# Moving four z tiles into the paired products, the norm products to VectorE and the norm rows to GpSimd's queue

## The chip, the cores and the metric

The kernel runs on one core of a Trainium2 chip. The metric is the device time of one execution in microseconds (us). A core has five engines that run side by side, each in the order of its own queue: TensorE (PE: matmuls, with PEld for its weight loads), VectorE (DVE), ScalarE (ACT), GpSimd (POOL) and SyncE (SP), which here only issues transfers (DMAs).

## The reference, cut to what matters

```python
u = rmsnorm(x) @ w_in                      # x: 1024 x 1024
z, xbc, dt_raw, s_b, s_c, s_x, g_a, g_b = split(u)     # z: 1024 x 2048
xbc = silu(conv4(xbc) + b);  xs, bm, cm = split(xbc)
y = ssd_chunked_scan(xs, softplus(dt_raw + dt_bias), a, bm, cm) + d_skip * xs
y = y * silu(z)
y = y * rsqrt(mean over each of 4 groups of 512 (y * y) + EPS) * ssd_norm_w
branch_a = y @ w_ssd_proj
branch_b = (s_b * conv3(s_c * s_x)) @ w_sconv_proj
h = x + (sigmoid(g_a) * branch_a + sigmoid(g_b) * branch_b) @ w_o
out = rmsnorm(h + swiglu(rmsnorm(h)))
```

All is float32. Each product is made of three matmuls (high by high, high by low, low by high) of rounded halves of both operands.

## The kernel before, in words

`u` is kept transposed: a tile is 128 columns of `w_in` by 1024 rows of `x`. Most tiles are made two at a time by a product of seven terms in place of eight (class `Pair`): a pair takes 7 slots of 4 matmul triples, 84 matmuls of 128x512, and leaves two tiles. The others, 6 tiles of z and the 16 gate tiles, are made one at a time in `direct_tile`: 2 halves of 8 triples, 48 matmuls a tile (lines L81 to L83, tile `pr`). The stages:

1. **Start.** The first four row tiles of `x` are loaded, squared and summed (L115, L117), scaled by their norm (L135, L137, tile `xn`), transposed on PE (L1542, tile `pt`), taken out of PSUM by `turned_out` (L1549 on ACT, L1551 on DVE, tile `br`) and split into high and low halves (L76, L77: `th`, `tl`). `cols` holds the small per-channel vectors; its copy is L1534.
2. **Pairs.** 29 pairs, 7 slots each (L679 to L681, tiles `pb` and `pd`). Ten of the 16 z tiles are here. A little way in, `d_skip_columns` (L1643) spreads the skip weights on DVE (L1644, `rd`) and transposes them on PE (L1646).
3. **Direct tiles and scan**, about 600 to 961 us. 22 direct tiles. Between their triples `pump_scan` puts the 65 steps of the scan (4 groups of 8 chunks, a step `part1` and a step `part2` for each), spread evenly over the triples by `due`. A step has small matmuls (`pxt`, `pcb`, `poff`, `pst`, `pdg`), a dozen DVE instructions and ACT's decays. Every four chunks a generator `norm` starts; it goes on by one `yield` at each scan step: it loads two tiles of silu(z) (L507), multiplies y by them (L513, on POOL), squares (L517, L518 on ACT: `sa`), adds (L520, L521 on DVE), sums over partitions on PE (L526, `pq`), takes the root (`rstd_of`, L99 to L107, with the square root on ACT, L101), transposes the result (L531, `prt`), copies it (L533, `rst`), writes it to memory (L535) and reads it back spread over 128 partitions (L537, `rbc`, from SP's queue), scales y by it (L543) and, for a second half, forms sums for the next product (L557).
4. **Merge.** Products of seven terms over weights and activations read back (class `Chunk`, `Stream`; `gb`, `gd` on PE; `split`, L73 to L77, makes `gh`, `gl`, `qh`, `ql`). The end of the last two norms runs beside its first chunks: after chunk 1, 2, 3 and 4 the program takes 4, 3, 0 and 3 scan steps.
5. The gated feed-forward and the last norm.

There is no scheduler: each engine's order is that of the program. Tiles come from a pool of 47 pages, and a load waits until the page's former content is read.

Of the kernel before, what the change touches and what calls it, by code (L numbers as in the profile page):

```python
# [10 lines left out]
AF = mybir.ActivationFunctionType  # L11
ALU = mybir.AluOpType

P = 128
S = 1024
D = 1024
# [23 lines left out]
def hybrid_block(ctx: ExitStack, tc: tile.TileContext, x, nmw, w_in, cw, cb, dtb, alog, dsk, snw,  # L40
                 wssd, scw, wsc, wo, nfw, wg, wu, wd, fnw, out):
    nc = tc.nc
    ET = mybir.EngineType
    ctx.enter_context(tc.manual_schedule(engines={ET.PE, ET.Activation, ET.DVE, ET.Pool, ET.SP}))
    x, w_in, out = x[0], w_in[0], out[0]
# [10 lines left out]
    def nm(s):  # L56
        cnt[0] += 1
        return f"{s}_{cnt[0]}"

    def page(s, shape=(P, 1024), dt=F32):  # L60
        return pp.tile(list(shape), dt, tag="pg", name=nm(s))

    def bank(s):
        return sm.tile([P, 512], F32, tag="sm", name=nm(s))
# [31 lines left out]
    def rstd_of(ssq, n, s):  # L96
        shp = list(ssq.shape)
        v = sp.tile(shp, F32, tag="rv", name=nm(s + "v"))
        nc.vector.tensor_scalar(v, ssq, 1.0 / n, EPS, op0=ALU.mult, op1=ALU.add)  # L99
        r = sp.tile(shp, F32, tag="rr", name=nm(s + "r"))  # L100
        nc.scalar.activation(r, v, AF.Sqrt)  # L101
        nc.vector.reciprocal(r, r)
        q = sp.tile(shp, F32, tag="rq", name=nm(s + "q"))
        nc.vector.tensor_mul(q, r, r)
        nc.vector.tensor_mul(q, q, v)
        nc.vector.tensor_scalar(q, q, -0.5, 1.5, op0=ALU.mult, op1=ALU.add)
        nc.vector.tensor_mul(r, r, q)  # L107
        return r
# [17 lines left out]
            rows_sq_on(e, acc, s)  # L126
        return acc

    def rows_scale(src, xn, ssq, act=(), pool=()):
        r = rstd_of(ssq, D, "n")  # L130
        for i in range(len(src)):
            if i in pool:
                nc.gpsimd.tensor_scalar(xn[i], src[i], r[:, i:i + 1], 1.0, op0=ALU.mult, op1=ALU.mult)
            elif i in act:
                nc.scalar.activation(xn[i], src[i], AF.Copy, scale=r[:, i:i + 1])  # L135
            else:
                nc.vector.tensor_scalar_mul(xn[i], src[i], r[:, i:i + 1])  # L137
        return xn

    def fill(rows, raw, half, wcol):  # L140
# [33 lines left out]
    def wslab(w, c0, cols=P, r0=0):  # L174
        return Slab(w[r0:r0 + D, c0:c0 + cols].rearrange("(k p) f -> p k f", p=P), (P, KT, cols))
# [45 lines left out]
    def every(gen):  # L221
        for _ in gen:
            pass
# [22 lines left out]
    d2 = cp.tile([16, 2], F32, name="d2")  # L246
# [9 lines left out]
    rd = cp.tile([16, 2, 64], F32, name="rd")  # L256
    cols = cp.tile([P, 192], F32, name="cols")
# [30 lines left out]
    V = nc.vector  # L288
# [213 lines left out]
    def norm(g, hf, y0, y1):  # L502

        ys, o = (y0, y1), slice(hf * 512, hf * 512 + 512)
        for i in range(2):
            z = page("z", HB)
            nc.sync.dma_start(z, z_g[g][256 * i:256 * i + 256, o].rearrange("(r p) l -> p r l", p=P))  # L507
            if i == 0:
                zs = z
        yield  # L510
        yield
        for y, z in zip(ys, (zs, z)):
            nc.gpsimd.tensor_mul(y, y, z)  # L513
        yield
        yield
        sa, sb = page("sa", HB), page("sa", HB)
        nc.scalar.activation(sa, y0, AF.Square)  # L517
        nc.scalar.activation(sb, y1, AF.Square)  # L518
        yield
        V.tensor_add(sa, sa, sb)  # L520
        V.tensor_add(sa[:, 0], sa[:, 0], sa[:, 1])  # L521
        yield
        yield
        pq = bank("pq")
        for c in range(4):
            nc.tensor.matmul(pq[:, c:c + 1], sa[:, 0, c * P:(c + 1) * P], ones, start=True, stop=True)  # L526
        rs = rstd_of(pq[:, 0:4], INNER // G, "g")
        yield
        yield
        prt = bank("prt")  # L530
        nc.tensor.transpose(prt[:4, :P], rs, ident)  # L531
        rst = sp.tile([4, P], F32, tag="rst", name=nm("rst"))
        nc.scalar.activation(rst, prt[:4, :P], AF.Copy)  # L533
        rd_ = rs_d[2 * g + hf]
        nc.sync.dma_start(rd_, rst)  # L535
        rbc = page("rbc", (P, 512))
        nc.sync.dma_start(rbc, rd_.rearrange("c l -> (c l)").partition_broadcast(P))  # L537
        yield
        yield
        yield  # L540
        for r in range(4):
            z = ys[r // 2][:, r % 2]
            V.scalar_tensor_tensor(z, z, snc(4 * g + r), rbc, op0=ALU.mult, op1=ALU.mult)  # L543
            if r % 2:
                yield
                if hf == 0 or r > 1:
                    nc.sync.dma_start(y_g[g][128 * (r - 1):128 * (r + 1), o].rearrange("(r p) l -> p r l", p=P),
                                      ys[r // 2])
        if hf == 0:
            kept[g] = ys  # L550
            return

        b11, b21 = kept.pop(g)
        b12, b22 = ys
        t1, t2 = page("s1", HB), page("s2", HB)
        for t, a, b, f in ((t1, b11, b12, "T1"), (t2, t1, b22, "T2"), (b12, b12, b22, "T3"), (b21, b21, t2, "T4")):
            V.tensor_add(t, a, b)  # L557
            nc.sync.dma_start(yt_d[f][256 * g:256 * g + 256, :].rearrange("(k p) f -> p k f", p=P), t)
            yield
# [50 lines left out]
    def silu_z(i):  # L610
        def f(u):
            nc.scalar.activation(u, u, AF.Silu)
            nc.scalar.dma_start(z_d[i], u)
            yield
        return f
# [290 lines left out]
                side.append(self.done[1](self.u2))  # L906
                self.u2 = self.b = None

    z_pairs = [Pair(i * P, (silu_z(i), silu_z(i + 1))) for i in range(0, 10, 2)]
    x_pairs = [Pair(XBC0 + i * P, (conv_silu(i), conv_silu(i + 1))) for g in range(G)  # L910
               for i in (4 * g, 4 * g + 2)]
    bc_pairs = [Pair(XBC0 + i * P, (conv_silu(i), conv_silu(i + 1))) for i in (16, 18, 20, 22)]
# [13 lines left out]
    NF = len(first)  # L926
# [33 lines left out]
    z_held = []  # L960

    def z_raw(i):
        def f(ps, hf):
            if hf == 0:
                z_held.append((i, page("gt")))
            nc.scalar.activation(z_held[-1][1][:, hf * 512:hf * 512 + 512], ps, AF.Copy)
            if hf and len(z_held) == 3:
                for k, t in z_held:
                    nc.scalar.activation(t, t, AF.Silu)
                    nc.scalar.dma_start(z_d[k], t)  # L970
                z_held.clear()
        return f

    direct = [(wslab(w_in, i * P), z_raw(i)) for i in range(10, 16)]
    for j in range(KT):
        direct += [(wslab(w_in, GA0 + j * P), gate_raw(ga_d[j])), (wslab(w_in, GB0 + j * P), gate_raw(gb_d[j]))]
    scan_steps = scans()
# [550 lines left out]
    a0 = rows_sq(xt[0:4], "x", "avav")  # L1528
    a1 = rows_acc(xt[4:8], "x")
    del xt  # L1530
    pc = bank("pc")
    nc.tensor.transpose(pc[:, 0:96], ra, ident[:96, :96])
    nc.tensor.transpose(pc[:, 96:176], rb, ident[:80, :80])
    nc.vector.tensor_copy(cols[:, 0:176], pc[:, 0:176])  # L1534
    r0 = rows_scale(*a0, act=(3,))
    raw0, raw1 = ([], []), ([], [])
    turned = {}

    def turn_rows(rows, k):
        pt = turned[k] = bank("pt")  # L1540
        for i in range(4):
            nc.tensor.transpose(pt[:, i * P:(i + 1) * P], rows[i][:, k * P:(k + 1) * P], ident)  # L1542

    def turned_out(raw, k):
        if k % 2 == 0:
            raw[k // 4].append(page("br", HB))
        o, pt = raw[k // 4][-1][:, k % 2, :], turned.pop(k)
        if k % 2 == 0:
            nc.scalar.activation(o, pt, AF.Copy, scale=nmc[:, k:k + 1])  # L1549
        else:  # L1550
            V.tensor_scalar_mul(o, pt, nmc[:, k:k + 1])  # L1551

    p0, p1, p2 = first
    for k in range(4):
        turn_rows(r0, k)
    turned_out(raw0, 0)
    turned_out(raw0, 1)
    p0.hi("A1")
    turned_out(raw0, 2)
    turned_out(raw0, 3)  # L1560
    p0.lo("A1")
# [78 lines left out]
            pump()  # L1640
    every(gen)

    def d_skip_columns():  # L1643
        V.tensor_copy(rd, d2.unsqueeze(2).to_broadcast([16, 2, 64]))  # L1644
        pd2 = bank("pd2")
        nc.tensor.transpose(pd2[:, 0:16], rd.rearrange("a b c -> a (b c)"), ident[:16, :16])  # L1646
        V.tensor_copy(cols[:, 176:192], pd2[:, 0:16])
# [3 lines left out]
    for i in range(7 * NF, n_slots):  # L1651
        slot(i)
        if i == 7 * NF + 4:
            time_steps(steps_ps)
            del steps_ps[:]
        if i == 7 * NF + 14:
            d_skip_columns()
        make(i)
        load_pairs((i + 11) // 7 + 1)
        pump()  # L1660
        if i % 3 == 0:
            next(sums, None)
        if i % 3 == 1:
            pump_aux()
        left = n_slots - 1 - i
        if left in (4, 3, 2):
            del T[{4: "T2", 3: "T1", 2: "T3"}[left]]
        if left == 9:
            b12 = [page("br", HB) for _ in range(2)]
            for k in range(2):  # L1670
                nc.sync.dma_start(b12[k], b12_d[k])
        if left == 7:
            direct[0][0].load()
        if left == 4:
            every(put("B12", b12))
        if left == 3:
            direct_hi(direct[0][0])
            direct[1][0].load()
        if left == 2:
            direct_lo(direct[0][0])  # L1680
            pump_scan()
# [42 lines left out]
```

## Time and profile before

| | us |
|---|---|
| median of 3 runs (lowest, highest) | 1929.16 (1929.04, 1929.68) |
| the profiled execution | 1931.04 |
| span of the profile, first to last instruction | 1929.3 |

A row of a group or a timeline names engine, line, operation, the tiles out<-in and the shape. In a timeline the two first numbers are start and duration in us, and what stands in brackets is the idle time ahead of it and what ended it. Matmuls overlap: the duration of one is longer than the distance to the next, so time on PE is counted by distances. Rows of waits give total, times and longest. A row of stretches gives for each engine its busy time in the stretch and the number of instructions.

### The profile page before, as it was taken

To read this page: it belongs to the slowest core of one execution; us is meant where nothing else is said; L and a number is where in the kernel's file an instruction comes from. 1 tells how busy PE (TensorE), PEld (TensorE's weight loads), DVE (VectorE), ACT (ScalarE), POOL (GpSimd) and SP (SyncE) were. 2 spreads that over 40 slices of the span, in tenths; PEclk is the share of its full clock that TensorE was granted. 3 is DMA by queue.
4 is the path that set the end of the run, shared out by engine and by line. 5 is a ranking of instruction groups with operands and counts; after the bars stand their busy time and mean duration, and the time that the engine had idled before them with its cause. 6 is when DMAs were issued, how large, how long until landed. Compare 5 with 4: busy or idle time off the path is not lost.

```text
span 1929.3 us, 24107 instructions
## 1 busy us (share of the span) xinstructions
PE 1887.9 (98%) x8917; PEld 1550.9 (80%) x8917; DVE 1291.1 (67%) x1660; ACT 965.0 (50%) x1533; POOL 181.4 (9%) x168
## 2 busy tenths in 40 slices
PE   7999999999999999999989999999999999999998
PEld 5688888888887888888868888887888888888886
DVE  7667878677774868887878548877444444456465
ACT  5545454444446877777546454465333333345333
POOL 1010111010100101010100000101221121100000
PEclk9999999999999999999989999999999999999999
DMA  5297999988959557768669766736998788867562
GB/s 179 62 260 170 242 233 232 229 207 227 272 138 289 189 180 252 246 220 275 209 243 373 233 222 203 207 125 133 227 205 208 199 192 200 217 259 287 193 196 109
DMA packets 345094, 411.97 MB, mean 214 GB/s; under 512 B 17192, under 2 KB 223744, under 8 KB 344976
## 3 DMA queue, kind: packets, MB, share of 16 engines
q1 hardware_dynamic: 293232, 325.39, 51.7%
q0 software_dynamic: 43680, 55.67, 18.2%
q10 hardware_dynamic: 8064, 29.36, 3.8%
q8 instruction: 70, 1.15, 0.2%
q14 instruction: 48, 0.39, 0.1%
HBM read 320.56 MB, written 143.15 MB: 240 GB/s over the span
## 4 chain that ended last, share of the span: by engine, by line
PE 87%; DVE 6%; ACT 3%; DMA 2%; issue 1%; SPq 0%; ACTq 0%; DVEq 0%
PE pb L679 5%; PE pb L680 5%; PE pb L681 5%; PE gb L680 5%; PE gb L679 5%; PE gb L681 5%; PE fb L681 4%; PE fb L679 4%; PE fb L680 4%; PE pr L81 4%; PE pr L83 4%; PE gd L679 4%; PE gd L680 4%; PE gd L681 4%; PE pr L82 4%; PE pd L679 4%
## 5 line engine op out<-in xcount | busy, mean ns | idle before, releaser
L77 DVE TENSOR_TENSOR wl<-ws,wh 128x1024 fp32r<-128x1024 f32 x77 | 94.0, 1222 | 121.5 <-ACT wh L76 121.5
L680 PE MATMUL gb<-ql,gh 128*128 128x512 f32 x432 | 169.7, 393 | 3.2 <-DVE ql L77 3.2
L679 PE MATMUL gb<-qh,gh 128*128 128x512 f32 x432 | 169.6, 393 | 1.1 <-DVE h L1132 1.1
L681 PE MATMUL gb<-qh,gl 128*128 128x512 f32 x432 | 169.3, 392 | 0.0
L81 PE MATMUL pr<-th,wh 128*128 128x512 f32 x352 | 144.2, 410 | 0.0
L83 PE MATMUL pr<-th,wl 128*128 128x512 f32 x352 | 138.2, 393 | 2.0 <-DVE wl L990 2.0
L681 PE MATMUL fb<-th,wl 128*128 128x512 f32 x352 | 137.2, 390 | 0.8 <-DVE wl L77 0.8
L679 PE MATMUL fb<-th,wh 128*128 128x512 f32 x352 | 137.3, 390 | 0.6 <-ACT wh L76 0.6
L82 PE MATMUL pr<-tl,wh 128*128 128x512 f32 x352 | 137.5, 391 | 0.0
L680 PE MATMUL fb<-tl,wh 128*128 128x512 f32 x352 | 137.1, 390 | 0.0
L679 PE MATMUL gd<-qh,gh 128*128 128x512 f32 x324 | 127.0, 392 | 0.0
L680 PE MATMUL gd<-ql,gh 128*128 128x512 f32 x324 | 126.7, 391 | 0.0
L681 PE MATMUL gd<-qh,gl 128*128 128x512 f32 x324 | 126.7, 391 | 0.0
L77 DVE TENSOR_TENSOR ql<-cb,qh 128x1024 fp32r<-128x1024 f32 x98 | 118.0, 1204 | 2.6 <-ACT qh L76 2.5
L76 ACT ACTIVATE qh<-cb 128x1024 fp32r<-128x1024 f32 x98 | 99.9, 1019 | 38.4 <-PE gb L680 17.2
L679 PE MATMUL fd<-th,wh 128*128 128x512 f32 x264 | 102.8, 390 | 0.0
L681 PE MATMUL fd<-th,wl 128*128 128x512 f32 x264 | 102.8, 390 | 0.0
L680 PE MATMUL fd<-tl,wh 128*128 128x512 f32 x264 | 102.8, 389 | 0.0
L74 DVE SCALAR_TENSOR_TENSOR gl<-ca,gh 128x1024 fp32r<-128x1024 f32 (+1 forms) x60 | 72.8, 1214 | 44.4 <-ACT gh L73 44.4
L680 PEld LDWEIGHTS gb<-ql,gh 128*128 128x128 f32 x432 | 81.8, 189 | 20.7 <-DVE ql L77 3.9
L679 PEld LDWEIGHTS gb<-qh,gh 128*128 128x128 f32 x432 | 81.8, 189 | 18.7 <-DVE h L1132 1.4
L681 PEld LDWEIGHTS gb<-qh,gl 128*128 128x128 f32 x432 | 81.9, 189 | 16.9
(319 smaller groups left out, 4681.7 us busy)
## 6 DMA issues: line engine op xcount, KB each, us to landing
ws<-in_w_in_dram SPq DMA_DIRECT2D x80, 512.0 KB, 7.1
ws<-in_w_gate_dram SPq DMA_DIRECT2D x77, 256.0 KB, 3.9
ws<-in_w_up_dram SPq DMA_DIRECT2D x77, 256.0 KB, 4.4
ca<-u_d SPq DMA_DIRECT2D x35, 512.0 KB, 5.5
ab<-ac_d SPq DMA_DIRECT2D x32, 512.0 KB, 6.9
xbc_g<-cv ACTq DMA_DIRECT2D x24, 512.0 KB, 7.0
ws<-ws POOLq DMA_DIRECT2D x22, 512.0 KB, 6.5
wd_d<-in_w_down_dram SPq DMA_DIRECT2D x20, 512.0 KB, 9.8
```

What stands on the lines that cost most here:

```text
L74: nc.vector.scalar_tensor_tensor(lo, src, -1.0, hi.bitcast(F32), op0=ALU.mult, op1=ALU.subtract)
L76: nc.scalar.activation(hi, src, AF.Copy)
L77: nc.vector.tensor_sub(lo, src, hi.bitcast(F32))
L81: nc.tensor.matmul(o, lh, rh, start=first, stop=False)
L82: nc.tensor.matmul(o, lh, rl, start=False, stop=False)
L83: nc.tensor.matmul(o, ll, rh, start=False, stop=last)
L679: nc.tensor.matmul(o, lh, rh, start=first, stop=False, skip_group_check=True)
L680: nc.tensor.matmul(o, lh, rl, start=False, stop=False, skip_group_check=True)
L681: nc.tensor.matmul(o, ll, rh, start=False, stop=last, skip_group_check=True)
```

## The change

Seven edits in one diff.

- `z_pairs` takes tiles 0 to 13 in place of 0 to 9: two more pairs (at the end of the pairs), four fewer direct tiles, 18. Only z tiles 14 and 15 stay direct, and their silu is done after two tiles instead of three (`z_raw`). The 65 scan steps are spread over the 18 tiles, since `due` goes by their number.
- In `norm` the product with silu(z) (L513) is on VectorE.
- In `norm` both transfers of the norm row (L535, L537) are issued from GpSimd's queue.
- In the start, `rows_scale` goes by column halves: first columns 0 to 511 of the four rows, then 512 to 1023.
- In the start, the copy of `cols` (L1534) is on ScalarE.
- In the start, the high half of the first weights (`p0.hi`, L864) stands ahead of the first two `turned_out`.
- `d_skip_rows` (the DVE copy L1644) is one slot ahead of `d_skip_columns`.

```diff
-    def rows_scale(src, xn, ssq, act=(), pool=()):
+    def rows_scale(src, xn, ssq, act=(), parts=1):
         r = rstd_of(ssq, D, "n")
-        for i in range(len(src)):
-            if i in pool:
-                nc.gpsimd.tensor_scalar(xn[i], src[i], r[:, i:i + 1], 1.0, op0=ALU.mult, op1=ALU.mult)
-            elif i in act:
-                nc.scalar.activation(xn[i], src[i], AF.Copy, scale=r[:, i:i + 1])
-            else:
-                nc.vector.tensor_scalar_mul(xn[i], src[i], r[:, i:i + 1])
+        for c in range(parts):
+            cs = slice(c * D // parts, (c + 1) * D // parts)
+            for i in range(len(src)):
+                if i in act:
+                    nc.scalar.activation(xn[i][:, cs], src[i][:, cs], AF.Copy, scale=r[:, i:i + 1])
+                else:
+                    nc.vector.tensor_scalar_mul(xn[i][:, cs], src[i][:, cs], r[:, i:i + 1])
         return xn
...
         for y, z in zip(ys, (zs, z)):
-            nc.gpsimd.tensor_mul(y, y, z)
+            V.tensor_mul(y, y, z)
...
-        nc.sync.dma_start(rd_, rst)
+        nc.gpsimd.dma_start(rd_, rst)
         rbc = page("rbc", (P, 512))
-        nc.sync.dma_start(rbc, rd_.rearrange("c l -> (c l)").partition_broadcast(P))
+        nc.gpsimd.dma_start(rbc, rd_.rearrange("c l -> (c l)").partition_broadcast(P))
...
-    z_pairs = [Pair(i * P, (silu_z(i), silu_z(i + 1))) for i in range(0, 10, 2)]
+    z_pairs = [Pair(i * P, (silu_z(i), silu_z(i + 1))) for i in range(0, 14, 2)]
...
-            if hf and len(z_held) == 3:
+            if hf and len(z_held) == 2:
...
-    direct = [(wslab(w_in, i * P), z_raw(i)) for i in range(10, 16)]
+    direct = [(wslab(w_in, i * P), z_raw(i)) for i in range(14, 16)]
...
-    nc.vector.tensor_copy(cols[:, 0:176], pc[:, 0:176])
-    r0 = rows_scale(*a0, act=(3,))
+    nc.scalar.activation(cols[:, 0:176], pc[:, 0:176], AF.Copy)
+    r0 = rows_scale(*a0, act=(3,), parts=2)
...
+    p0.hi("A1")
     turned_out(raw0, 0)
     turned_out(raw0, 1)
-    p0.hi("A1")
     turned_out(raw0, 2)
     turned_out(raw0, 3)
     p0.lo("A1")
...
+    def d_skip_rows():
+        V.tensor_copy(rd, d2.unsqueeze(2).to_broadcast([16, 2, 64]))
+
     def d_skip_columns():
-        V.tensor_copy(rd, d2.unsqueeze(2).to_broadcast([16, 2, 64]))
...
+        if i == 7 * NF + 13:
+            d_skip_rows()
         if i == 7 * NF + 14:
             d_skip_columns()
```

How the order moves at the three places that the prediction speaks of. First VectorE where the merge begins: `gl` and `ql` are the low halves for its second and third chunk, `y_7640` and `y_7641` are the y of the last norm, `y_7175` that of the one before. Before:

```order
L107 TENSOR_TENSOR gr_8123<-gr_8123,gq_8126 128x4
L557 TENSOR_TENSOR y_6719<-y_6719,y_6720 128x1024
L74 SCALAR_TENSOR_TENSOR gl_8178<-ca_7882,gh_8177 128x1024
L77 TENSOR_TENSOR ql_8182<-cb_7884,qh_8181 128x1024
L77 TENSOR_TENSOR gl_8186<-ca_8032,gh_8185 128x1024
L77 TENSOR_TENSOR ql_8190<-cb_8034,qh_8189 128x1024
L557 TENSOR_TENSOR y_6256<-y_6256,s_1231_8078 128x1024
L543 SCALAR_TENSOR_TENSOR y_7175<-y_7175,cols,rbc_8228 128x512 x2
L520 TENSOR_TENSOR sa_8232<-sa_8232,sa_8233 128x1024
```

The same place of the changed kernel, in which the last norm's y are `y_7691` and `y_7692`, and `y_7250` is that of the one before:

```order
L107 TENSOR_TENSOR gr_8138<-gr_8138,gq_8141 128x4
L557 TENSOR_TENSOR y_6819<-y_6819,y_6820 128x1024
L74 SCALAR_TENSOR_TENSOR gl_8190<-ca_7864,gh_8189 128x1024
L77 TENSOR_TENSOR ql_8194<-cb_7866,qh_8193 128x1024
L77 TENSOR_TENSOR gl_8198<-ca_8044,gh_8197 128x1024
L77 TENSOR_TENSOR ql_8202<-cb_8046,qh_8201 128x1024
L557 TENSOR_TENSOR y_6388<-y_6388,s_1237_8096 128x1024
L513 TENSOR_TENSOR y_7691<-y_7691,z_8146 128x1024
L513 TENSOR_TENSOR y_7692<-y_7692,z_8148 128x1024
L543 SCALAR_TENSOR_TENSOR y_7250<-y_7250,cols,rbc_8240 128x512 x2
L520 TENSOR_TENSOR sa_8244<-sa_8244,sa_8245 128x1024
```

The two products stand between the splits of the third chunk and the scaling that waits for the norm row. Second, SP's queue at the same time: `ca` and `cb` are the merge's operands, `yt_d` takes the last of the sums (L557), and `rs_d_138` and `rbc_8228` are the norm row of the norm before the last. Before:

```order
L741 DMA cb_8175<-vt_d_160 128x2x512
L558 DMA yt_d_166<-y_6256 128x2x512
L535 DMA rs_d_138<-rst_8225 4x128
L537 DMA rbc_8228<-rs_d_138 128x512
L741 DMA ca_8240<-sc_d_144 128x2x512
L741 DMA cb_8242<-vt_d_160 128x2x512
```

GpSimd's queue of the changed kernel from the same norm to the first instruction of the feed-forward (`ws`):

```order
L535 DMA rs_d_138<-rst_8237 4x128
L537 DMA rbc_8240<-rs_d_138 128x512
L535 DMA rs_d_139<-rst_8401 4x128
L537 DMA rbc_8404<-rs_d_139 128x512
L1239 DMA ws_10141<-in_w_gate_dram 128x4x128
```

The norm row no longer stands behind the store of y, and the loads of the merge no longer behind the norm row. Third, ScalarE at the start: `xn_213` is the fourth row tile, `wh` the high half of the first weights, `br` and `th` the transposed rows and their high halves. Before:

```order
L101 ACTIVATE nr_222<-nv_220 128x4
L135 ACTIVATE xn_213<-x_88,nr_222 128x1024
L1549 ACTIVATE br_254<-pt_234,cols 128x512
L864 ACTIVATE wh_257<-ws_183 128x1024
L1549 ACTIVATE br_260<-pt_244,cols 128x512
L76 ACTIVATE th_284<-br_254 128x1024
```

And of the changed kernel:

```order
L1534 ACTIVATE cols<-pc_216 128x176
L101 ACTIVATE nr_222<-nv_220 128x4
L135 ACTIVATE xn_213<-x_88,nr_222 128x512 x2
L864 ACTIVATE wh_258<-ws_183 128x1024
L1549 ACTIVATE br_261<-pt_238,cols 128x512
L1549 ACTIVATE br_264<-pt_248,cols 128x512
L76 ACTIVATE th_288<-br_261 128x1024
```

The weights' half stands ahead of both transposed tiles, and the copy of `cols`, which was on VectorE ahead of the root, is here.

## The prediction

> **What bounds the kernel now.** I read the page first, then PE's waits, then the stretches of the scan stage, then the timelines of the two places where PE stands.
>
> ```profile
> span 1929.3 us, 24107 instructions
> PE 1887.9 (98%) x8917; PEld 1550.9 (80%) x8917; DVE 1291.1 (67%) x1660; ACT 965.0 (50%) x1533; POOL 181.4 (9%) x168
> L81 PE MATMUL pr<-th,wh 128*128 128x512 f32 x352 | 144.2, 410 | 0.0
> PE pc L1532 <- DMA ra<-in_ssd_conv_w_dram: 7.4, 1, 7.4
> PE pq L526 <- DVE sa L521: 6.4, 1, 6.4
> PE gb L680 <- DVE ql L77: 3.2, 1, 3.2
> PE pr L83 <- DVE wl L990: 2.0, 3, 1.1
> PE pd L1646 <- DVE rd L1644: 0.8, 1, 0.8
> 300.00:400.00 100.00, 100.00 (x441) 82.58 (x441) 75.62 (x86) 44.27 (x58) 8.82 (x10) 1.00 0.83 203
> 600.00:720.00 120.00, 116.58 (x689) 94.54 (x688) 78.22 (x129) 97.29 (x222) 11.36 (x5) 1.00 0.65 204
> 720.00:961.00 241.00, 241.00 (x1472) 199.10 (x1471) 201.27 (x336) 172.29 (x398) 24.81 (x10) 1.00 0.73 240
> 961.00:1000.00 39.00, 29.45 (x112) 23.52 (x112) 25.26 (x28) 18.37 (x23) 5.70 (x2) 0.82 0.74 255
> ```
>
> PE bounds: it is busy for 98% and a matmul starts every 100/441 = 0.227 us. It stands only at the start and at 961 to 1000, where 112 matmuls take the time of 39/0.227 = 172: some 13 us are lost there, part of it to a granted clock of 0.82. The scan stage is full on PE, but VectorE is at 201.3 of 241 us in its main stretch, so it is next.
>
> **The change, part by part.** The sum is made on the profiled execution: 1931.0 us in all, span 1929.3. The runs' median, 1929.2, has no profile; I carry the difference over to it.
>
> *Matmuls.* Four direct tiles are 4 x 48 = 192 (the group shows 352 = 22 x 16 for one of three lines), two pairs are 2 x 84 = 168. 24 fewer at 0.227: **-5.4**. The pair stage grows by 38.1, the scan stage loses 43.5.
>
> ```profile
> 500.00:600.00 100.00, 100.00 (x442) 82.60 (x441) 72.84 (x84) 44.92 (x59) 10.36 (x12) 1.00 0.81 216
> ```
>
> What a pair needs beside its matmuls (sums and splits on VectorE, halves and evictions on ScalarE, two loads of 512 KB) is costed at nothing: the last 100 us of pairs keep PE full with VectorE at 73% and ScalarE at 45%, and four z tiles have no convolution, which most pairs there carry. Were that cover gone, a pair would take as long as VectorE's work on it, still under its 19 us of matmuls by the same row.
>
> *Start.*
>
> ```profile
> 11.96 2.08 DVE L137 TENSOR_SCALAR xn<-x,nr 128x1024 f32<-128x1024 f32 x3
> 14.10 4.90 PE L1542 MATMUL pt<-ident,xn 128*128 128x128 f32 x30 [0.19 <-DVE xn L137]
> 17.29 0.75 DVE L1551 TENSOR_SCALAR br<-pt,cols 128x512 f32<-128x512 f32 x1 [0.86 <-PE pt L1542]
> 20.36 0.50 PE L680 MATMUL pb<-tl,wh 128*128 128x512 f32 x1 [1.13 <-DVE tl L77]
> 19.84 0.42 ACT L1512 ACTIVATE wdt<-wdts 128x256 fp32r<-128x256 f32 x1 [0.65 <-DMA wdts<-in_w_in_dram]
> 10.27 0.34 DVE L1534 COPY cols<-pc 128x176 f32<-128x176 f32 x1
> ```
>
> Three whole rows take VectorE 2.08 us, so the three first halves are there after about 1.04, and the transposes run through 1.0 earlier; the copy that leaves VectorE gives 0.3 more; the weights' half on ScalarE fills its wait instead of standing between tiles. So PE's 20.36 comes 1.3 to 1.7 earlier. But `wdts` still lands at 19.84, and ScalarE stops there with all that follows. Kept to the end: 0.6 to 1.7, taken **-1.0**.
>
> *Skip rows.* The copy goes a slot ahead; its wait (0.8) goes, and VectorE has the same work: **-0.8**, at worst 0.
>
> *Waits at direct tiles.* PE waited three times for `wl`, 2.0 in all; one ACT silu group of three is now one of two, the other gone. 0 to 2.0, taken **-0.5**.
>
> *End of the norms, 961 to 1000.*
>
> ```profile
> 963.56 3.47 DVE L74 SCALAR_TENSOR_TENSOR gl<-ca,gh 128x1024 fp32r<-128x1024 f32 x1 [4.12 <-ACT gh L73]
> 966.95 3.37 DVE L77 TENSOR_TENSOR ql<-cb,qh 128x1024 fp32r<-128x1024 f32 x1
> 970.24 1.21 DVE L77 TENSOR_TENSOR gl<-ca,gh 128x1024 fp32r<-128x1024 f32 x1
> 963.53 5.70 POOL L513 TENSOR_TENSOR y<-y,z 128x1024 f32<-128x1024 f32 x2 [33.34 <-ACT gh L73]
> 967.01 0.27 ACT L533 ACTIVATE rst<-prt 4x128 f32<-4x128 f32 x1 [0.64 <-PE prt L531]
> 973.75 0.36 SPq L558 DMA_DIRECT2D yt_d<-y  x1
> 974.21 0.32 SPq L535 DMA_DIRECT2D rs_d<-rst  x1
> 981.55 1.41 DVE L543 SCALAR_TENSOR_TENSOR y<-y,cols,rbc 128x512 f32<-128x512 f32 x2 [7.82 <-DMA rbc<-rs_d]
> 984.97 1.84 PE L526 MATMUL pq<-ones,sa 128*128 128x1 f32 x8 [6.38 <-DVE sa L521]
> ```
>
> While POOL multiplies, two VectorE splits take 3.47 and 3.37 instead of 1.21: 4.4 us, and PE's 3.2 wait behind `ql`. With the products on VectorE, behind these splits, that goes. Then the norm row: ready at 967.3, it waited in SP's queue for a store until 974.21, and VectorE had it 7.3 later. From GpSimd, which has nothing else queued, it leaves at 967.3. How long that queue takes for it no row shows:
>
> ```profile
> ra<-in_ssd_conv_w_dram POOLq DMA_DIRECT2D x1, 48.0 KB, 5.5
> ws<-in_w_up_dram POOLq DMA_DIRECT2D x22, 256.0 KB, 8.0
> ```
>
> The ends are SP's own 7.3 and 5.5 + 8.0 = 13.5 by POOL's rows. I take 8.5, near the first, for the transfer is the same, and the second row's is one that adds up. So `rbc` at 975.8 (974.6 to 980.8), and `pq` 3.4 later as now, at 979.2 instead of 984.97: -5.8; half a microsecond back for VectorE's two products ahead of it: **-5.3** (-0.7 to -7.3). A wait of PE remains here, since its second chunk, no longer held, ends near 972: some 7 us, with its price in clock.
>
> ```profile
> 970.96 0.63 PE L681 MATMUL gb<-qh,gl 128*128 128x512 f32 x1
> 971.39 0.63 PE L679 MATMUL gb<-qh,gh 128*128 128x512 f32 x1
> ```
>
> After the first wait the matmuls go at 0.43 instead of 0.227 for a while; that loss lies before `pq` and goes with the wait. After `pq` I leave it as it is, since a wait of about the same length stands ahead of it in both kernels.
>
> The Trainium skill's "DMA: Bandwidth & Descriptors", section "SWDGE vs HWDGE vs iDMA", speaks against this edit: plain transfers belong on SP or ACT, where hardware makes the descriptors. By its first-byte figures (about 1 and 0.6 us, section "Specifications") two transfers would cost 0.8 more than on SP, an estimate of 8.1 in place of my 8.5; no run here shows it yet.
>
> In the other norms GpSimd waits for `rst` with nothing queued behind it, and SP, which had waited there, is free.
>
> *VectorE in the scan stage.* 16 products come to VectorE's queue, 14 of them in this stage, and a product now holds back all scan work behind it if its z is late.
>
> ```profile
> L513 POOL TENSOR_TENSOR y<-y,z 128x1024 f32<-128x1024 f32 x16 | 41.0, 2584 | 323.9 <-DMA z<-z_g 175.1 <-DVE y L496 39.5 <-DVE wl L990 39.3
> L557 DVE TENSOR_TENSOR s<-y,y 128x1024 f32<-128x1024 f32 x4 | 4.9, 1218 | 0.0
> 925.00 5.20 POOL L513 TENSOR_TENSOR y<-y,z 128x1024 f32<-128x1024 f32 x2 [36.63 <-DMA z<-z_g]
> 927.27 3.21 DVE L496 TENSOR_TENSOR y<-y,xx 128x256 f32<-128x256 f32 x2
> 919.58 0.76 DVE L496 TENSOR_TENSOR y<-y,xx 128x256 f32<-128x256 f32 x2
> DVE gr L102 <- ACT gr L101: 19.3, 6, 4.3
> DVE xx L437 <- PE pxt L426: 8.0, 5, 2.9
> ```
>
> Z is in time: POOL starts at 925.00, and VectorE reaches this place only after 927.27. The stretch of 241 us shrinks with the stage, (361 - 43.5)/361, to 212. VectorE's work in it: 201.3, less 2.4 (3.21 against 0.76) for each pair of products that collides, taken for three of the five pairs, -7.4, plus ten products at 1.2, +12, less three weight splits, -3.6: 202, or 95%. In line with it stand 19.3 us of waits for ScalarE's square root; with them 222, 10 over. PE's waits for a scan step's state come only when VectorE is two steps, 2 x 212/43 = 10 us, behind (65 steps in 317 us, 43 here). So between 0 and 10 us reach PE; taken **+2**, near the low end, since VectorE starts this stretch with 78.2 of 120 us used.
>
> Sum: -5.4 - 1.0 - 0.8 - 0.5 - 5.3 + 2 = -11.0, so 1929.2 - 11.0 = **1918.2**.
>
> **The rivals.**
>
> *All covers hold.* VectorE stays ahead and every term is at its good end: -5.4 - 1.7 - 0.8 - 2.0 - 7.3 = -17.2: 1912. For it: PE had no wait at all in the 241 us, and VectorE's collisions may have cost more than the 7.4 I took off. Against it: the 222 needs the whole lag of 10 to stay hidden.
>
> *VectorE gives the matmuls back.* It falls 8 us behind instead of 2: -5.0, 1924.2. For it: the 222 against 212.
>
> *GpSimd's queue is as slow as its rows.* 13.5 instead of 8.5: the end gives 0.7 instead of 5.3: -6.4, 1922.8. Against it: those transfers met full queues.
>
> *Both:* -0.4, 1928.8, no change.
>
> *Slower: VectorE bounds the scan stage.* If all its idle time (241 - 201.3 = 39.7) is order of work and moves along, it needs 202 + 39.7 = 242 where PE has 212, so 30 come on top of -13.0: 1946. It decides from 17 us of PE waits in this stage. Against it: part of the idle time was waiting for PE (`pxt`, 8.0), which goes when VectorE is late.
>
> **How the numbers follow.** Forecast 0.48, all covers 0.17, matmuls back 0.14, slow queue 0.08, both 0.06, slower 0.07. A measurement tells about 0.2%, 3.9 us. The first four are faster by more (0.87), both is within (0.06), the last slower (0.07). The range leaves out these last two, 0.13, and a little of the far end of the covers: 1911.5 to 1924.5.
>
> **What would show it.** Matmuls with `pr` 864 instead of 1056. VectorE's `gl` and `ql` at the merge's begin at 1.2 us each; `pq` there with a wait of 3 to 7, some 6 us sooner after the first `gb`; `rs_d` and `rbc` 8 to 9 us from `rst` to VectorE. VectorE over 90% busy in the scan stage, its wait for `pxt` nearly gone, and PE's waits there for `st`, `xw` or `wl` some 2 us. The first `tl` matmul near 19. Wrong if PE's waits in the scan stage pass 8 us, or if the norm row takes over 12.

## The result and the profile after

| us | before | after |
|---|---|---|
| median (lowest, highest) of 6 runs each | 1929.84 (1929.04, 1931.28) | 1942.72 (1939.96, 1943.55) |
| the profiled execution | 1931.04 | 1939.96 |
| span of the profile | 1929.3 | 1938.2 |

The ratio is 1.0064, interval 1.0051 to 1.0077. The forecast was 1918.2, so the kernel is 12.9 us slower where 11 less were expected. The profiled execution is the quickest of the six; the working below is made on its span, 8.9 above that of before.

The head of the page of after, and the group of one of the three lines of direct tiles:

```profile
span 1938.2 us, 24072 instructions
PE 1886.9 (97%) x8893; PEld 1547.4 (80%) x8893; DVE 1304.7 (67%) x1698; ACT 966.2 (50%) x1540; POOL 149.0 (8%) x168
L81 PE MATMUL pr<-th,wh 128*128 128x512 f32 x288 | 120.3, 418 | 0.0
```

The matmuls did go: 288 = 18 x 16 for each line, 24 fewer on PE in all. But PE is busy for nearly as long, 1886.9 against 1887.9, in a span that is 8.9 longer. Where it stands now, from PE's waits in the whole of after, without those of the start:

```profile
PE pq L526 <- DVE sa L521: 11.2, 2, 9.2
PE prt L531 <- DVE gr L107: 5.4, 4, 2.4
PE pr L83 <- DVE wl L990: 3.8, 1, 3.8
PE poff L475 <- DVE st L484: 2.1, 1, 2.1
```

Every one of them names VectorE (two smaller ones, 1.1 and 0.9, name ScalarE). Three of the four lie in the scan stage, and so do 2.0 of the first; before, all listed waits of PE between 637 and 961 came to 0.5. The stretches of after from the first direct tile (637) to the first `gb` (974) and beyond show when it happens:

```profile
637.00:760.00 123.00, 122.13 (x756) 99.81 (x755) 91.58 (x157) 104.47 (x251) 1.13 (x2) 1.00 0.63 206
760.00:880.00 120.00, 113.84 (x700) 92.47 (x699) 104.00 (x179) 86.59 (x207) 3.21 (x6) 0.99 0.71 231
880.00:974.00 94.00, 85.63 (x518) 69.72 (x517) 79.07 (x137) 62.19 (x144) 2.13 (x4) 0.95 0.70 228
974.00:1000.00 26.00, 16.80 (x70) 13.67 (x69) 16.78 (x22) 12.93 (x18) 1.06 (x2) 0.80 0.73 268
```

PE is full until 760. From there it loses 6.2 of 120 and 8.4 of 94 us, and the granted clock falls to 0.95 in the last stretch. VectorE is not full in either: 104.0 of 120, 79.1 of 94. What VectorE stood for in the scan stage, first in the kernel before (600 to 961):

```profile
DVE gr L102 <- ACT gr L101: 23.6, 7, 4.3
DVE xx L437 <- PE pxt L426: 21.8, 11, 5.5
```

and in after (637 to 975):

```profile
DVE gr L102 <- ACT gr L101: 23.6, 7, 4.3
DVE y L543 <- DMA rbc<-rs_d: 10.8, 4, 4.1
DVE xx L437 <- PE pxt L426: 9.4, 4, 5.9
```

`gr` is the wait for the square root: seven times in both, 23.6 in both. The wait for `pxt` is the one that shows VectorE ahead of PE: 21.8 before, 9.4 now. And 10.8 for the norm row are new; before, it had none there. One root in after, in the middle of the stage:

```profile
798.16 0.16 DVE L99 TENSOR_SCALAR gv<-pq 128x4 f32<-128x4 f32 x1
...
798.85 1.06 ACT L400 ACTIVATE ab<-ab 128x1024 f32<-128x1024 f32 x1
...
799.93 1.28 ACT L101 ACT_TABLE_LOAD   x1
...
801.22 0.20 ACT L101 ACTIVATE gr<-gv 128x4 f32<-128x4 f32 x1
...
801.46 0.18 DVE L102 RECIPROCAL gr<-gr 128x4 f32<-128x4 f32 x1 [3.14 <-ACT gr L101]
...
802.48 0.27 PE L531 MATMUL prt<-ident,gr 128*4 128x128 f32 x1 [1.88 <-DVE gr L107]
```

VectorE hands the mean over at 798.3 and then does nothing for 3.14 us: ScalarE is in the middle of a scan step's decays, then loads the table of the root (1.28), then takes the root (0.20). All of VectorE's later scan work stands behind that, and PE, which has reached `prt` by then, stands for 1.88.

The merge of after, VectorE, ScalarE, GpSimd and PE:

```profile
976.17 1.23 DVE L74 SCALAR_TENSOR_TENSOR gl<-ca,gh 128x1024 fp32r<-128x1024 f32 x1 [2.63 <-ACT gh L73]
977.31 1.22 DVE L77 TENSOR_TENSOR ql<-cb,qh 128x1024 fp32r<-128x1024 f32 x1
979.62 0.27 ACT L533 ACTIVATE rst<-prt 4x128 f32<-4x128 f32 x1 [0.64 <-PE prt L531]
980.18 0.51 POOL L535 DMA_DIRECT2D rs_d<-rst  x1 [28.88 <-ACT rst L533]
985.57 0.55 POOL L537 DMA_DIRECT2D rbc<-rs_d  x1 [4.88 <-PE gb L681]
990.82 1.41 DVE L543 SCALAR_TENSOR_TENSOR y<-y,cols,rbc 128x512 f32<-128x512 f32 x2 [6.62 <-DMA rbc<-rs_d]
994.24 1.84 PE L526 MATMUL pq<-ones,sa 128*128 128x1 f32 x8 [9.20 <-DVE sa L521]
```

The splits run at 1.2 and PE no longer waits for `ql`, as forecast. The row leaves 0.3 after `rst` instead of 6.9, but takes 10.9 from `rst` to VectorE where 8.5 was forecast. The groups of its two transfers:

```profile
rbc<-rs_d POOLq DMA_DIRECT2D x8, 256.0 KB, 4.0
rs_d<-rst POOLq DMA_DIRECT2D x8, 2.0 KB, 4.8
```

The read back over 128 partitions takes what it took on SP (4.0; 4.2 before). It is the write of 2 KB that is dear: 4.8 from issue to landing. Before, SP issued the read, which waits for that write, some 1.2 us after the write in six of the eight norms.

By stages, from the first direct `pr`, the first `gb` and the `pq` behind it:

| us | before | after | forecast of the difference | measured |
|---|---|---|---|---|
| start to first `pr` | 600.1 | 637.3 | +38.1 - 1.8 = +36.3 | +37.2 |
| scan stage, first `pr` to first `gb` | 361.2 | 336.5 | -43.5 - 0.5 + 2 = -42.0 | -24.7 |
| `gb` to `pq` | 23.7 | 20.4 | -5.3 | -3.3 |
| `pq` to the end | 944.3 | 943.9 | 0 | -0.4 |

17.3 of the 19.9 us between forecast and result are in the scan stage.

### The profile page after: what moved, and what is told of

The parts are those of the page before. It is cut to its first block, busy times and chain, and to the rows that moved or that the text cites. A ratio compares the mean times of both kernels' runs of the same rounds, so it can differ in the third digit from the quotient of the medians.

```text
span 1938.2 us, 24072 instructions
## 1 busy us (share of the span) xinstructions
PE 1886.9 (97%) x8893; PEld 1547.4 (80%) x8893; DVE 1304.7 (67%) x1698; ACT 966.2 (50%) x1540; POOL 149.0 (8%) x168
## 3 DMA queue, kind: packets, MB, share of 16 engines
q0 software_dynamic: 44576, 57.79, 18.8%
## 4 chain that ended last, share of the span: by engine, by line
PE 80%; DVE 8%; ACT 6%; issue 3%; DMA 2%; SPq 0%; ACTq 0%; POOL 0%; DVEq 0%; POOLq 0%
PE pb L679 5%; PE pb L680 5%; PE pb L681 5%; PE gb L680 5%; PE gb L679 5%; PE gb L681 5%; PE fb L681 4%; PE fb L679 4%; PE fb L680 4%; PE pd L679 4%; PE pd L680 4%; PE pd L681 4%; PE gd L679 4%; PE gd L681 4%; PE gd L680 4%
## 5 line engine op out<-in xcount | busy, mean ns | idle before, releaser
L81 PE MATMUL pr<-th,wh 128*128 128x512 f32 x288 | 120.3, 418 | 0.0
L83 PE MATMUL pr<-th,wl 128*128 128x512 f32 x288 | 114.6, 398 | 3.8 <-DVE wl L990 3.8
L82 PE MATMUL pr<-tl,wh 128*128 128x512 f32 x288 | 113.7, 395 | 0.0
L679 PE MATMUL pb<-th,wh 128*128 128x512 f32 x248 | 97.6, 393 | 0.8 <-ACT u L894 0.8
L680 PE MATMUL pb<-tl,wh 128*128 128x512 f32 x248 | 96.9, 391 | 1.3 <-DVE tl L77 1.3
L679 PE MATMUL pb<-th,wk 128*128 128x512 f32 x248 | 96.7, 390 | 0.7 <-ACT th L76 0.4
```

The source lines that it names most:

```text
L81: nc.tensor.matmul(o, lh, rh, start=first, stop=False)
L82: nc.tensor.matmul(o, lh, rl, start=False, stop=False)
L83: nc.tensor.matmul(o, ll, rh, start=False, stop=last)
L679: nc.tensor.matmul(o, lh, rh, start=first, stop=False, skip_group_check=True)
L680: nc.tensor.matmul(o, lh, rl, start=False, stop=False, skip_group_check=True)
```

## The experiments

Times are medians; in each round the kernel before ran on the same chip: 1930.96 in the first (e1 to e4), 1930.08 in the second (e5 to e8), 1930.45 in the third (e9 to e12). Ratios are against these, with their intervals.

**First round: which edit.** Two theories stood after the comparison above. The row theory: the norm row on GpSimd's queue comes so late that VectorE stands for it in the middle of the scan (the 10.8). The load theory: VectorE has too much to do, sixteen products included, for a stage that is 43.5 us shorter.

*e1, rows back on SP.*

```diff
-        nc.gpsimd.dma_start(rd_, rst)
+        nc.sync.dma_start(rd_, rst)
...
-        nc.gpsimd.dma_start(rbc, rd_.rearrange("c l -> (c l)").partition_broadcast(P))
+        nc.sync.dma_start(rbc, rd_.rearrange("c l -> (c l)").partition_broadcast(P))
```

> The changed kernel with both transfers of the norm row back on SP's queue, all else as changed. Row theory (the row's way through GpSimd's queue is some 4 us longer at its write, VectorE stands at the scaling for it, 21 us in all, and PE behind VectorE): the waits of VectorE for rbc inside the scan stage go to under 4 us, the scan stage falls from 336 us to 318 to 324, and the time to 1921 to 1930. Load theory (four direct tiles fewer are too short for VectorE's work, whichever queue the row takes): the stage stays above 332 us and the time above 1937.

1934.4 (10 runs), ratio 1.002, 1.0011 to 1.0029, which lies in neither theory's range. 8.3 come back, nearly all in the scan stage (328.3 instead of 336.5). The rest of the loss stays: the stage should be 314 by the matmuls (361.2, less 3.4 in which PE stood at its beginning before, less 43.5). PE's waits in e1's scan stage are fewer, but they are the same kind:

```profile
PE poff L475 <- DVE st L484: 3.3, 1, 3.3
PE prt L531 <- DVE gr L107: 2.9, 3, 1.5
```

*e2, products back on GpSimd, rows left there.*

```diff
-            V.tensor_mul(y, y, z)
+            nc.gpsimd.tensor_mul(y, y, z)
```

> The changed kernel with the norm products back on GpSimd, rows still on its queue. Row theory: the waits for rbc stay, the stage stays near 336 us, the time 1938 to 1946. A product theory (in VectorE's order the products delay what stands behind them): the stage falls below 325 us, the time to about 1930.

1958.93 (4 runs), ratio 1.0148, 1.0131 to 1.0165: 16 us worse than after, with a stage of 355.1; neither forecast came out. So the products on VectorE are no loss. The run decides nothing on the load theory: with fewer instructions in its queue VectorE was busy for longer. One reason can be read from one group, L496 on VectorE, in before, in after and in e2:

```profile
L496 DVE TENSOR_TENSOR y<-y,xx 128x256 f32<-128x256 f32 x56 | 30.0, 576 | 1.0
```

```profile
L496 DVE TENSOR_TENSOR y<-y,xx 128x256 f32<-128x256 f32 x56 | 21.3, 422 | 1.0
```

```profile
L496 DVE TENSOR_TENSOR y<-y,xx 128x256 f32<-128x256 f32 x56 | 42.6, 802 | 1.0
```

576 ns in the mean with GpSimd's products beside it, 422 without, 802 in e2. The other reason is GpSimd's queue. In e2 the products stand in it behind the row's transfers, and in seven of the eight norms they begin as soon as the row's read is issued, as here:

```profile
732.95 0.57 POOL L535 DMA_DIRECT2D rs_d<-rst  x1 [37.39 <-ACT rst L533]
736.55 0.58 POOL L537 DMA_DIRECT2D rbc<-rs_d  x1 [3.03 <-PE poff L475]
737.15 4.75 POOL L513 TENSOR_TENSOR y<-y,z 128x1024 f32<-128x1024 f32 x2
```

e4 below has products on GpSimd too, with rows on SP; there the same products begin at 725.3, and the kernel is 19 us faster than e2. So most of e2's loss is the two together in one queue.

*e3, ten tiles of z in the pairs again, all else as after.*

```diff
-    z_pairs = [Pair(i * P, (silu_z(i), silu_z(i + 1))) for i in range(0, 14, 2)]
+    z_pairs = [Pair(i * P, (silu_z(i), silu_z(i + 1))) for i in range(0, 10, 2)]
...
-            if hf and len(z_held) == 2:
+            if hf and len(z_held) == 3:
...
-    direct = [(wslab(w_in, i * P), z_raw(i)) for i in range(14, 16)]
+    direct = [(wslab(w_in, i * P), z_raw(i)) for i in range(10, 16)]
```

> The changed kernel with ten z tiles in the pairs and 22 direct tiles as before, all other edits kept. Row theory and load theory alike: with 361 us for the stage VectorE has slack, its waits for rbc are at most 1 to 2 us a norm and PE does not see them; what is left is the start, the skip rows and the end of the norms, 1924 to 1928. Were the waits for rbc enough by themselves to hold PE, the time would be 1932 or more.

1926.12 (10 runs), ratio 0.998, 0.997 to 0.9989. With 22 direct tiles the other edits are worth 4.8. And VectorE stands for the row in this stage just as long as in after, 10.9 us in three. That is not quite free: the stage takes 365.2 in the profiled execution, the slowest of the ten, and PE waits 4.1 for `wl` in it.

*e4, the kernel before with the four tiles of z moved and nothing else* (the same three lines, the other way, in before).

> The kernel before with the four z tiles moved and nothing else. Load theory: the shorter stage is too short for VectorE, PE waits more than 10 us in it, the time is 1936 or more. Row theory: the row on SP's queue is 5 us on its way and just fits three shorter scan steps, PE waits under 4 us in the stage, the time is 1923 to 1928.

1939.89 (4 runs), ratio 1.0052, 1.0037 to 1.0067. The move that takes 24 matmuls away makes the kernel 9 us slower by itself, as the load theory had it. So the loss sits in the shortened stage, and the row adds to it there: +9 for z, -5.5 for products and start (e1 against e4), +8.3 for the row.

**Second round: what in the shortened stage.** Neither theory says why e1 still loses 14 us in a stage in which VectorE is busy for 274.7 of 328.3. The root theory: VectorE's wait in line for ScalarE's root is the loss; with 22 tiles VectorE is ahead of PE and the wait is hidden, with 18 it is not. The rival, the ScalarE theory: ScalarE's own queue delivers late, and what VectorE does meanwhile makes no difference.

*e5, rows on SP, the root cut in two.* `norm` writes out what `rstd_of` did, with a scan step between ScalarE's root and VectorE's use of it, in place of one of the two that came behind:

```diff
-        rs = rstd_of(pq[:, 0:4], INNER // G, "g")
-        yield
+        rv = sp.tile([P, 4], F32, tag="rv", name=nm("gv"))
+        V.tensor_scalar(rv, pq[:, 0:4], 1.0 / (INNER // G), EPS, op0=ALU.mult, op1=ALU.add)
+        rs = sp.tile([P, 4], F32, tag="rr", name=nm("gr"))
+        nc.scalar.activation(rs, rv, AF.Sqrt)
+        yield
+        V.reciprocal(rs, rs)
+        q = sp.tile([P, 4], F32, tag="rq", name=nm("gq"))
+        V.tensor_mul(q, rs, rs)
+        V.tensor_mul(q, q, rv)
+        V.tensor_scalar(q, q, -0.5, 1.5, op0=ALU.mult, op1=ALU.add)
+        V.tensor_mul(rs, rs, q)
         yield
```

(From here on the lines behind L527 are 9 higher in the kernels that carry this: `gb` is L688 to L690, `prt` L540, the scaling by `rbc` L552.)

> The changed kernel with the rows on SP's queue, and the root of each norm cut in two: VectorE hands the mean to ScalarE in one scan step and takes the square root from it in the next, in place of standing for it; the number of steps of a norm stays. In the runs so far VectorE is busy 275 of the 328 to 337 us of the stage and stands 24 us for the root. Root theory (VectorE is not full, it stands in line for ScalarE's root and all scan work behind stands with it): this wait falls under 4 us, the stage falls from 328.3 to 314 to 321 us, the time to 1920 to 1926. ScalarE theory (ScalarE's own queue is what is late, the root is only where VectorE meets it): VectorE's wait moves to the next thing it takes from ScalarE, the stage stays above 325 us, the time above 1931.

1921.88 (4 runs), ratio 0.9955, 0.994 to 0.997: 12.5 us less than e1 with the same work, and the fastest kernel so far. The same root as above, in e5:

```profile
795.91 0.16 DVE L528 TENSOR_SCALAR gv<-pq 128x4 f32<-128x4 f32 x1
795.99 0.69 DVE L476 TENSOR_TENSOR xx<-poff,eb 128x512 f32<-128x512 f32 x1
...
798.97 0.21 ACT L530 ACTIVATE gr<-gv 128x4 f32<-128x4 f32 x1
...
799.31 0.17 DVE L532 RECIPROCAL gr<-gr 128x4 f32<-128x4 f32 x1
...
800.33 0.27 PE L540 MATMUL prt<-ident,gr 128*4 128x128 f32 x1 [0.37 <-DVE gr L537]
```

ScalarE is as late with it as before, 3.1 us after `gv`; VectorE goes on with L476 at once and comes back without a wait, and PE's wait shrinks from 1.88 to 0.37. One stretch of the stage in e1 (first) and in e5:

```profile
760.00:880.00 120.00, 116.53 (x729) 95.21 (x728) 108.44 (x186) 91.93 (x222) 0.00 (x0) 0.99 0.75 245
```

```profile
760.00:880.00 120.00, 119.63 (x756) 98.58 (x755) 112.38 (x195) 95.25 (x227) 0.00 (x0) 1.00 0.79 258
```

VectorE does more in the same time (112.4 of 120) and PE is full. So at 18 direct tiles the load theory falls as well as the ScalarE theory: VectorE can carry that load, if it need not stand in line.

*e6, the changed kernel as it is, with the root cut* (the diff of e5 alone; rows on GpSimd).

> The changed kernel as it is, rows on GpSimd's queue, with the root cut in two. Root theory: the stage falls from 336.5 to 320 to 329 us, the waits for rbc stay, the time is 1926 to 1934. ScalarE theory: above 333 us, 1939 or more. Should the rows alone be what holds VectorE, nothing changes either: 1940.

1922.81 (4 runs), ratio 0.9958, 0.9943 to 0.9973. 19.9 less than after, from one scan step between two instructions, and better than any theory's time. The stage is 320.0, where the prediction's terms put it at 319.2. In the whole the row on GpSimd costs 0.9 now, less than the intervals can tell, against 8.3 with the root in one piece. It is not free in the stage, where VectorE stands 7.8 for it and which is 4.9 longer than e5's; the merge, 2.1 shorter, and the stretches around give most of that back.

*e7, ten tiles of z, rows on SP* (e1 and e3 together).

> 22 direct tiles as before and the rows on SP's queue: of the change there are left the products on VectorE, the start and the skip rows. With ten z tiles and the rows on GpSimd's queue the stage was 365.3 us with 5 us of PE waits for wl behind the rows. Root theory and ScalarE theory alike: the stage is 359 to 362 us, the time 1920 to 1925. If the products on VectorE cost something at 22 tiles, the stage is above 363 us.

1926.62 (10 runs), ratio 0.9981, 0.9971 to 0.9991, with a stage of 360.3; the time is 1.6 above the range. The medians of the four kernels with the root in one piece make a table in which the row's queue matters in one column only. (By stages it shows in both: e3's profiled stage is 4.9 longer than e7's, with 1.9 of it back at the merge, and that execution was 3.2 above e3's median.)

| us | 22 direct tiles | 18 direct tiles |
|---|---|---|
| rows on SP | 1926.62 (e7) | 1934.4 (e1) |
| rows on GpSimd | 1926.12 (e3) | 1942.72 (after) |

*e8, e1 without the products.* It leaves out the product of y with silu(z) and keeps all else, the loads of z too.

```diff
-        for y, z in zip(ys, (zs, z)):
-            V.tensor_mul(y, y, z)
```

> The changed kernel with the rows on SP's queue and the products with silu(z) left out (y goes into the norm without them). Takes 16 us of work from VectorE in the stage and leaves every wait in its place. Root theory: PE is later than VectorE's line by less, the stage falls from 328.3 to 315 to 322 us. ScalarE theory: above 325 us.

A single time of 1932.7 with a span of 1930.9, against e1's span of 1932.5. Sixteen products of 1.2 are gone, which takes some 15 us from VectorE's work in the stage (259.3 busy against 274.7), and the stage is 2.2 shorter (326.1 against 328.3). Here the root theory's forecast failed; the ScalarE theory had the stage above 325. In the same stretch of e8:

```profile
760.00:880.00 120.00, 115.98 (x722) 94.80 (x722) 102.11 (x180) 92.28 (x222) 0.00 (x0) 0.99 0.74 244
```

VectorE has 6 us less to do than in e1, and PE is no fuller there. Work that is taken out is not what PE waits for; e5 took out a wait and gained 12.5. Why so little of the 15 us arrives is argued only: the waits for `bh` and `pxt` grow by some 10 us in its place, since VectorE then reaches the next result of ScalarE or PE earlier and stands for that. So what VectorE stands for counts in this stage, and by this run its total of work does not.

**Third round: where the cut counts, and what is next.**

*e9, the kernel before with the root cut.*

> The kernel before with one edit: the root cut in two scan steps. Root theory: with 22 direct tiles VectorE is ahead of PE in the scan stage and its wait in line for the root (23.6 us in that kernel too) is hidden, so nothing changes: ratio 0.999 to 1.001, 1928 to 1932. Rival, a fixed price: the cut saves its 12 to 13 us at any length of the stage, as a root late in VectorE's line delays every step behind it: 1917 to 1920.

1932.19 (10 runs), ratio 1.0011, 1.0001 to 1.002. No gain: 1.7 slower, 0.2 to 3.9 by the interval, a hair outside the root theory's range and far from the rival's. The 23.6 us in line cost nothing with 22 direct tiles; they are not a fixed price. In their place VectorE stands for PE: its wait for `pxt` (L437) is 28.9 there in 18, where it was 21.8 in 11.

*e10, the kernel before with four tiles of z and the cut.*

> The kernel before with the four tiles of z moved and the root cut, products still on GpSimd and rows on SP. Root theory: the same kernel with the root in one piece took 1939.9, 12 to 13 less gives 1927 to 1928. Rival, the products: with GpSimd multiplying beside VectorE the shortened stage stays too tight even without the wait in line, and the time stays above 1932.

1928.94 (10 runs), ratio 0.9993, 0.9984 to 1.0003. 11 less than e4, so the cut is worth about as much with GpSimd's products as with VectorE's; it ends a little above the 1927 to 1928 of the root theory. What is left against e5, 7.1, is the other edits: 5.2 of it is in the scan stage (320.3 against 315.1), where GpSimd's products still slow VectorE (474 ns for L496, against 602 in e4 and 422 without them).

*e11, e5 with the younger norm stepped first.*

```diff
-            for n in list(norms):
+            for n in list(norms)[::-1]:
```

At the merge of e5 the sums of the last norm stand behind the scaling of the one before it, which waits for the row:

```profile
967.47 0.34 SPq L546 DMA_DIRECT2D rbc<-rs_d  x1
...
972.07 1.42 DVE L552 SCALAR_TENSOR_TENSOR y<-y,cols,rbc 128x512 f32<-128x512 f32 x2 [8.73 <-DMA rbc<-rs_d]
973.40 1.22 DVE L520 TENSOR_TENSOR sa<-sa,sa 128x1024 f32<-128x1024 f32 x1
...
975.49 1.84 PE L526 MATMUL pq<-ones,sa 128*128 128x1 f32 x8 [11.31 <-DVE sa L521]
```

> The changed kernel with rows on SP, the root cut, and at each scan step the younger norm stepped before the older, so that at the merge the last norm's sums (L520, L521) stand ahead of the scaling that waits for the row (L552 there). Path theory: PE's wait of 11.3 for pq was VectorE standing 8.73 for the row with those sums behind it; it goes, and with it the loss of clock behind it: 1910 to 1917. Rival: the wait only moves along, as the scaled tiles are then late for the following products, or the root of the last norm is: 1920 to 1923.

1914.14 (4 runs), ratio 0.9914, 0.9899 to 0.9929: the fastest kernel of this study, 28.6 below after and 16.3 below before. The same place in e11:

```profile
962.47 1.23 DVE L520 TENSOR_TENSOR sa<-sa,sa 128x1024 f32<-128x1024 f32 x1
...
964.56 1.02 PE L526 MATMUL pq<-ones,sa 128*128 128x1 f32 x8 [1.26 <-DVE sa L521]
...
968.88 1.41 DVE L552 SCALAR_TENSOR_TENSOR y<-y,cols,rbc 128x512 f32<-128x512 f32 x2 [4.47 <-DMA rbc<-rs_d]
```

VectorE still stands for the row (4.47), but PE's wait is 1.26 instead of 11.31. `pq` comes 12.4 after the first `gb` instead of 22.5; 3.4 of the 10 are lost again behind it, where a `gd` now waits 2.6 for the next `gv`.

*e12, e5 with all sixteen tiles of z in the pairs* (only the 16 gate tiles are direct).

> The changed kernel with rows on SP, the root cut, and all sixteen tiles of z in the pairs, so that only the 16 gate tiles are direct. Root theory: the stage becomes 22 us shorter, about 296 to 299, and VectorE's 275 us of work still fit: 12 matmuls fewer give -2.7, 1918 to 1920. Rival, the load: with VectorE at 93% what is left of its waits (bh, pxt) comes out at PE: 1923 to 1935.

1930.43 (10 runs), ratio 1.0, 0.9991 to 1.001: 8.5 worse than e5 with 12 matmuls fewer. Here the forecast of the root theory failed, and the time is in the range of the load theory. PE's wait for the norm, of which 8.7 in five lie in the scan stage, and the stretch that was full in e5:

```profile
PE prt L540 <- DVE gr L537: 12.6, 6, 3.9
```

```profile
760.00:880.00 120.00, 114.69 (x729) 94.02 (x728) 111.93 (x193) 93.38 (x224) 0.00 (x0) 0.99 0.74 244
```

VectorE is busy for 112 of 120 us in both; its own waits between are those for ScalarE and PE. The stage takes 312.7, hardly less than e5's 315.1 with two tiles more. PE's largest wait is again for the root's way through VectorE and ScalarE, now with the cut. Whether it is VectorE's work or such round trips that set this floor, no run separates.

## Why the prediction was wrong

The rival that came about is the slower one, at 0.07: waits that were "order of work" did move along, at 1942.7 against its 1946. Its point, 17 us of PE waits in the stage, was nearly met: 15.3 are listed (5.4, 3.8, 2.1, 2.0 and two small ones of 1.1 and 0.9). The stage is some 22 longer than its matmuls ask for; the rest goes with the fallen clock. But that VectorE is full is not what the runs show for 18 tiles: it is busy for 275 of the 336.5 us, 82% where the prediction's sign was over 90%. e8 takes some 15 us of work away and gains 1.6 on the span, e5 takes the wait away and gains 12.5.

- *Matmuls, -5.4: right.* 24 fewer, the pair stage 37.2 longer with the start's gain in it. When the wait in line is gone (e5) the scan stage is 315.1, against the 314 that the matmuls ask for.
- *Start and skip rows, -1.8: half.* The first `tl` matmul came 1.3 sooner (19.09), but from 39 us on 0.4 of it was left. The skip rows' wait is gone. Together they gave 0.9.
- *Waits at direct tiles, -0.5: wrong sign.* One wait of 3.8 for `wl` in place of three that made 2.0. VectorE splits that weight late: with the rows on SP (e1) the wait is 0.3.
- *End of the norms, -5.3: mis-sized,* 3.3. The mechanism was right (no collision, the row leaves at once, PE's wait for `ql` gone), the row took 10.9 in place of 8.5. (The ends of this term's range do not follow from its own times, which give -0.8 and -7.0 before the half microsecond; no reading hangs on that.) My sentence on the Trainium skill, "DMA: Bandwidth & Descriptors", section "SWDGE vs HWDGE vs iDMA", had the direction: plain transfers belong on SP or ACT. The trace agrees, but by more than the estimate of 8.1 from its first-byte figures: the eight rows took 8.7 to 12.1 from `rst` to VectorE, which stood waiting for six of them.
- *"In the other norms GpSimd waits for `rst` with nothing queued behind it": true, and beside the point.* Who waits for the row is VectorE, with the whole scan behind it. Before, VectorE reached L543 8.6 to 11.0 after `rst` and never waited in the scan stage; that was 2.0 to 5.6 after the row had landed. On GpSimd's queue VectorE had to wait for it in four of the stage's six norms. I priced this edit at the merge alone. In the scan stage it costs 8.2 with the root in one piece (after against e1) and 4.9 with the root cut (e6 against e5). With the merge counted in, it costs next to nothing in the medians of e6 against e5 and of e3 against e7.
- *VectorE in the scan stage, +2: this step failed.* It counted the right things, work 202 and 19.3 in line against 212, and found them 10 over. Then it let the 10 vanish in a lag of two scan steps, and took the value near the low end. Measured, this term and the one for the direct tiles gave 18.8 in place of 1.5. With the root cut and nothing else (e6) the stage falls from 336.5 to 320.0, and the forecast had it at 319.2: the wait in line for the root, which the term let vanish, is nearly the whole miss. The lag was not there to hide it. PE's waits name first not a scan step's state but the norm's own `prt` (5.4 in four), two steps behind `pq`, with a round trip from VectorE to ScalarE and back within them. That the rest of the loss comes by way of the scan work behind the root, rather than by VectorE's total of work, fits e8 but is not shown step by step.
- *The clock:* with the waits the granted clock fell, to 0.95 in the last stretch of the stage, where the full stretches of before and e5 have 1.00. No term held that for this stage.

## What to carry to other kernels

Before a stage is shortened for the engine that bounds it, put the next engine's waits in line beside its work, and ask of each what hides it now: here 23.6 us of standing for a square root were free as long as VectorE ran ahead, and cost 12 us when the stage lost 43.5. Such a wait is cut by program order: start the other engine's step one step earlier and take its result later (e6, 19.9 us for a `yield`), or put work that another engine waits for ahead of the waiting instruction (e11). A slower queue for a short chain of transfers costs nothing until the reader arrives first; from then on the reader's wait has to be followed to the bounding engine, where it cost 8.2 us of the stage here and 4.9 in e6.

## What the runs showed of the hardware

- A write of 2 KB from GpSimd's queue took 4.8 us from issue to landing, in the median of eight, where SP's queue had the dependent read issued 1.2 us after the write in six of eight; on SP, too, that distance went to 5.9 at the merge of e5.
- The same VectorE instruction of two inputs, 128x256, took 422 ns in the mean without products on GpSimd, 576 in the kernel before and 802 in e2, with GpSimd multiplying beside it.
- In after, waits of PE of up to 3.8 us each in the scan stage went with a granted clock of 0.95 in its last stretch, against 1.00 in the stretch of e5 without them.
